# One head row of batch 0 loaded early by SyncE in place of two, in a rotary embedding kernel

## The chip, the cores and the metric

The kernel runs on one core of one Trainium2 chip. The metric is the device time of one execution in microseconds (us); the time of a kernel is the median over several runs.

## The reference

Each pair of halves of a head is rotated by an angle given per position. Everything is float32.

```python
def setup_inputs():
    batch, seq_len, num_heads, head_dim = (8, 2048, 16, 64)
    # x: (8, 2048, 16, 64), cos and sin: (2048, 32), normal draws
def reference(x, cos, sin):
    x1, x2 = x[..., :32], x[..., 32:]
    cos, sin = cos[None, :, None, :], sin[None, :, None, :]
    out1 = x1 * cos - x2 * sin
    out2 = x1 * sin + x2 * cos
    return np.concatenate([out1, out2], axis=-1)
```

The input and the output are 67.1 MB each, so that the kernel moves about 134 MB and does three multiplications or additions for each element.

## The kernel before, in words

The 2048 positions of a batch are spread over 128 partitions with J = 16 consecutive positions in each. One position of one partition, here called a **row**, has 16 heads of 64 elements, that is 4 KB in float32 and 2 KB in float16. A batch is 16 rows in each partition, 64 KB of float32.

The data is kept in float16 in `buf`, five batches deep (NBUF = 5). GpSimd (POOL) issues nearly all transfers, since its software-described DMAs convert between float32 in memory and float16 in `buf`: `load` (the issue is line 71) and `store` (line 81). `in_ring` ties them into one program order, and they all go through one software queue, q0 in the profile, which works first in, first out. A transfer becomes one DMA packet per partition and batch, spread over 16 DMA engines, 8 packets on each, and one closing semaphore packet per engine.

`rotate` (lines 83 to 100) does three VectorE (DVE) operations on a stretch of rows in float16: v = swapped halves times signed sine (line 92), buf = buf times cosine (line 98), buf = buf + v (line 100).

The order of the program is written out by hand (lines 102 to 141):

- SyncE (SP) loads the sine table (line 41) and then the first JA = 2 rows of batch 0, unconverted, into the float32 tile `head` (line 42). ScalarE (ACT) loads the cosine table (line 40). These are hardware-described DMAs, q1 for SP and q10 for ACT.
- POOL issues `load(0)`, which takes rows JA to 15 of batch 0, and `load(1)`.
- ACT converts the tables to float16 (lines 104 to 106) and copies `head` into rows 0 and 1 of `buf` (line 107).
- DVE rotates rows 0 to JA of batch 0 (line 111); POOL stores row 0 alone (line 112), then issues `load(2, 2)` (batches 2 and 3) and `load(4)`.
- DVE rotates the other rows of batch 0 (line 115), and POOL stores rows 1 to 15 (line 116). Batches 1 to 7 follow. A load of batch 5, 6 or 7 waits for the store that frees its buffer.
- At the end, the last two rows of batch 7 leave in another way: ACT copies them to float32 in the same tile `head` (line 134), and SP stores them unconverted (line 135) once the store of rows 0 to 8 of that batch has landed.

Of the kernel before, what the change touches and what calls it, by code (L numbers as in the profile page):

```python
# [1 line left out]

# [4 lines left out]


@with_exitstack  # L10
def kernel(
    ctx: ExitStack,
    tc: tile.TileContext,
    x: bass.AP,
    cos: bass.AP,
    sin: bass.AP,
    out: bass.AP,
):
    nc = tc.nc
    f16 = mybir.dt.float16  # L20
    f32 = mybir.dt.float32

    B, S, H, D = x.shape
    Dh = D // 2
    P = nc.NUM_PARTITIONS
    J = S // P
    NBUF = 5

    const_pool = ctx.enter_context(tc.tile_pool(name="rope_const", bufs=1))
    io_pool = ctx.enter_context(tc.tile_pool(name="rope_io", bufs=1))  # L30
    tmp_pool = ctx.enter_context(tc.tile_pool(name="rope_tmp", bufs=1))

    JA = 2
    head = const_pool.tile([P, JA, H, D], f32)
    x0 = x[0].rearrange("(p j) h d -> p j (h d)", j=J)
    sin_f = const_pool.tile([P, J, Dh], f32)
    cos_f = const_pool.tile([P, J, Dh], f32)
    cos_h = const_pool.tile([P, J, Dh], f16)
    sin_h = const_pool.tile([P, J, D], f16)
    nc.scalar.dma_start(out=cos_f, in_=cos.rearrange("(p j) d -> p j d", j=J))  # L40
    nc.sync.dma_start(out=sin_f, in_=sin.rearrange("(p j) d -> p j d", j=J))
    nc.sync.dma_start(
        out=head.rearrange("p j h d -> p (j h d)"),
        in_=x0[:, 0:JA, :].rearrange("p j f -> p (j f)"),
    )

    buf = io_pool.tile([P, NBUF, J, H, D], f16)

    ring = []

    def in_ring(dma):
        if ring:
            tc.add_manual_dep(
                dma.ins,
                ring[-1].ins.name,
                mybir.DependencyInfo(mybir.DependencyClass.NoSync, mybir.DependencyReason.DATA),
                reason="order of the ring",
            )
        ring.append(dma)
        return dma  # L60

    def load(b, n=1):
        k = b % NBUF
        if n == 1:
            j0 = JA if b == 0 else 0
            dst = buf[:, k, j0:J, :, :].rearrange("p j h d -> p (j h d)")
            src = x[b].rearrange("(p j) h d -> p j (h d)", j=J)[:, j0:J, :].rearrange("p j f -> p (j f)")
        else:
            dst = buf[:, k : k + n, :, :, :].rearrange("p b j h d -> p b (j h d)")
            src = x[b : b + n].rearrange("b (p j) h d -> p b (j h d)", j=J)  # L70
        in_ring(nc.gpsimd.dma_start(out=dst, in_=src))  # L71

    def store(b, n=1, j0=0, j1=J):
        k = b % NBUF
        if n == 1:
            src = buf[:, k, j0:j1, :, :].rearrange("p j h d -> p (j h d)")
            dst = out[b].rearrange("(p j) h d -> p j (h d)", j=J)[:, j0:j1, :].rearrange("p j f -> p (j f)")
        else:
            src = buf[:, k : k + n, :, :, :].rearrange("p b j h d -> p b (j h d)")
            dst = out[b : b + n].rearrange("b (p j) h d -> p b (j h d)", j=J)  # L80
        return in_ring(nc.gpsimd.dma_start(out=dst, in_=src))  # L81

    def rotate(b, j0=0, j1=J):
        v = tmp_pool.tile([P, J, H, D], f16)
        n = j1 - j0
        js = slice(j0, j1)
        xt = buf[:, b % NBUF, js, :, :]
        shape = [P, n, H, 2, Dh]
        sin_b = sin_h[:, js, :].rearrange("p j (e d) -> p j e d", e=2).unsqueeze(2).to_broadcast(shape)
        cos_b = cos_h[:, js, :].unsqueeze(2).to_broadcast([P, n, 2 * H, Dh])  # L90
        xe = xt.rearrange("p j h (e d) -> p j h e d", e=2)
        nc.vector.tensor_mul(  # L92
            out=v[:, js, :, :].rearrange("p j h (e d) -> p j h e d", e=2),
            in0=xe[:, :, :, ::-1, :],
            in1=sin_b,
        )
        xw = xt.rearrange("p j h (e d) -> p j (h e) d", d=Dh)
        nc.vector.tensor_mul(out=xw, in0=xw, in1=cos_b)  # L98
        xa = xt.rearrange("p j h d -> p (j h d)")
        nc.vector.tensor_add(out=xa, in0=xa, in1=v[:, js, :, :].rearrange("p j h d -> p (j h d)"))  # L100

    load(0)
    load(1)
    nc.scalar.copy(out=sin_h[:, :, Dh:D], in_=sin_f)  # L104
    nc.scalar.mul(out=sin_h[:, :, 0:Dh], in_=sin_f, mul=-1.0)  # L105
    nc.scalar.copy(out=cos_h, in_=cos_f)  # L106
    nc.scalar.copy(  # L107
        out=buf[:, 0, 0:JA, :, :].rearrange("p j h d -> p (j h d)"),
        in_=head.rearrange("p j h d -> p (j h d)"),
    )  # L110
    rotate(0, 0, JA)
    store(0, 1, 0, 1)
    load(2, 2)
    load(4)
    rotate(0, JA, J)
    store(0, 1, 1, J)
    rotate(1)
    store(1)
    rotate(2)
    store(2)  # L120
    load(5, 2)
    load(7)
    rotate(3)
    rotate(4)
    store(3, 2)
    rotate(5)
    rotate(6)
    store(5, 2)
    rotate(7)
    gate = store(7, 1, 0, 9)  # L130
    store(7, 1, 9, J - JA)
    last = buf[:, 7 % NBUF, J - JA : J, :, :].rearrange("p j h d -> p (j h d)")
    dst = out[B - 1].rearrange("(p j) h d -> p j (h d)", j=J)[:, J - JA : J, :].rearrange("p j f -> p (j f)")
    nc.scalar.copy(out=head.rearrange("p j h d -> p (j h d)"), in_=last)  # L134
    end = nc.sync.dma_start(out=dst, in_=head.rearrange("p j h d -> p (j h d)"))
    tc.add_manual_dep(
        end.ins,
        gate.ins.name,
        mybir.DependencyInfo(mybir.DependencyClass.Sync, mybir.DependencyReason.DATA),
        reason="the last rows go out behind this part",  # L140
    )


# [1 line left out]
_INS = ['x', 'cos', 'sin']  # L145
_OUTS = [((8, 2048, 16, 64), 'float32')]


# [23 lines left out]
```

## Time and profile before

| what | value |
|---|---|
| time, median of 3 runs | 316.54 us (316.42 to 316.58) |
| the profiled execution: its own time | 316.39 us |
| its span in the profile | 314.6 us |
| DVE busy | 209.1 us, 27 operations |
| ACT busy | 6.7 us |
| POOL busy | 8.6 us |
| HBM read and written | 67.63 MB and 67.11 MB, 428 GB/s over the span |

The profile shows one execution. The span runs from the first to the last event that the profiler recorded; 1.8 us of the execution lie around it. A page gives, for 40 equal slices of the span (7.87 us each), the busy share of each engine in tenths, and the busy share of the core's 16 DMA engines as "DMA". Its bytes per DMA queue count what arrives: float16 for a load of `buf`, float32 for a store. The timeline gives each instruction's start, duration, engine, line and tiles; a DMA issue there is only the issuing instruction, the transfer itself follows later. Windows give the DMA busy share of a stretch, where a packet is put down whole to the window in which it starts. A share above 1 is therefore a window in which many packets start, and a share of 0 is one in which none starts because all engines are still in their packets. Behind these views the trace holds one record per DMA packet, with its queue, start, duration and bytes.

### The profile page before, as it was taken

The numbers are of one execution on the slowest core, as the hardware profiler recorded it, in microseconds if no ns is written. First come the engines' busy times: TensorE is split into PE (matmuls) and PEld (weight loads), VectorE is DVE, ScalarE is ACT, GpSimd is POOL, SyncE is SP. The second block draws the span as 40 slices with busy tenths as digits, with TensorE's granted clock in tenths as the row PEclk, the third lists the DMA queues.
The fourth block names the chain that finished last, engine by engine and source line by source line (L and its number), as shares of the span: only waits on it lengthen the run. The fifth ranks groups of instructions, "written<-read, shape, count | busy, mean of one in ns | idle before, by whom it ended". The sixth has DMA issues, their size and how long they took to land.

```text
span 314.6 us, 114 instructions
## 1 busy us (share of the span) xinstructions
DVE 209.1 (66%) x27; ACT 6.7 (2%) x6; POOL 8.6 (3%) x18
## 2 busy tenths in 40 slices
DVE  0039999992499999999950000899999999910000
ACT  3200000000000000000000000000000000020000
POOL 1020000000000000000010000000000000010000
DMA  7999999999999899999999999999999999999998
GB/s 240 252 242 200 200 267 200 200 267 200 200 200 325 375 500 400 400 400 533 400 200 221 246 200 200 246 221 333 400 508 425 400 400 525 408 400 400 433 425 342
DMA packets 3104, 101.71 MB, mean 323 GB/s; under 512 B 288, under 2 KB 288, under 8 KB 672
## 3 DMA queue, kind: packets, MB, share of 16 engines
q0 software_dynamic: 2528, 99.09, 98.1%
q1 hardware_dynamic: 432, 2.36, 1.9%
q10 hardware_dynamic: 144, 0.26, 0.2%
HBM read 67.63 MB, written 67.11 MB: 428 GB/s over the span
## 4 chain that ended last, share of the span: by engine, by line
DVE 65%; another core or an unknown queue 15%; DMA 7%; ACT 1%; issue 0%; DVEq 0%; ACTq 0%; PEldq 0%
DVE buf L98 22%; DVE v L92 22%; DVE buf L100 22%; DMA buf<-in_x_dram 7%; ACT head L134 1%; DVEq L92 0%; ACTq L134 0%; PEldq L167 0%
## 5 line engine op out<-in xcount | busy, mean ns | idle before, releaser
L92 DVE TENSOR_TENSOR v<-buf,sin_h 128x16384 f16<-128x16384 f16 (+2 forms) x9 | 69.7, 7744 | 66.6 <-DMA buf<-in_x_dram 51.3
L98 DVE TENSOR_TENSOR buf<-buf,cos_h 128x16384 f16<-128x16384 f16 (+2 forms) x9 | 69.7, 7744 | 0.3
L100 DVE TENSOR_TENSOR buf<-buf,v 128x16384 f16<-128x16384 f16 (+2 forms) x9 | 69.7, 7744 | 0.3
L81 POOL DMA_DIRECT2D out_dram<-buf x8 | 4.7, 584 | 219.2 <-DVE buf L100 219.2
L134 ACT CAST head<-buf 128x2048 f32<-128x2048 f16 x1 | 1.9, 1897 | 261.3 <-DVE buf L100 261.3
L71 POOL DMA_DIRECT2D buf<-in_x_dram x6 | 3.7, 628 | 49.7 <-DMA out_dram<-buf 48.9
L107 ACT CAST buf<-head 128x2048 f16<-128x2048 f32 x1 | 1.9, 1897 | 7.1 <-DMA head<-in_x_dram 7.1
L104 ACT ACT_TABLE_LOAD x1 | 1.3, 1283 | 1.2 <-PEq L156 1.2
L104 ACT CAST sin_h<-sin_f 128x512 f16<-128x512 f32 x1 | 0.6, 617 | 2.0 <-DMA sin_f<-in_sin_dram 2.0
L105 ACT ACTIVATE sin_h<-sin_f 128x512 f16<-128x512 f32 x1 | 0.6, 624 | 0.0
L106 ACT CAST cos_h<-cos_f 128x512 f16<-128x512 f32 x1 | 0.6, 601 | 0.0
L156 POOL MEMSET const-float32-0.0<- 128x1 f32 x1 | 0.1, 98 | 0.2 <-issue 0.2
L156 POOL MEMSET const-bfloat16-1.0<- 128x1 bf16 x1 | 0.1, 101 | 0.0
L156 POOL MEMSET const-uint8-127<- 128x1 uint8 x1 | 0.1, 99 | 0.0
L156 POOL MEMSET const-float32-1.0<- 128x1 f32 x1 | 0.1, 98 | 0.0
## 6 DMA issues: line engine op xcount, KB each, us to landing
buf<-in_x_dram POOLq DMA_DIRECT2D x2, 8192.0 KB, 60.3
buf<-in_x_dram POOLq DMA_DIRECT2D x3, 4096.0 KB, 57.4
out_dram<-buf POOLq DMA_DIRECT2D x1, 7680.0 KB, 73.5
out_dram<-buf POOLq DMA_DIRECT2D x1, 4608.0 KB, 28.6
buf<-in_x_dram POOLq DMA_DIRECT2D x1, 3584.0 KB, 22.5
out_dram<-buf POOLq DMA_DIRECT2D x1, 2560.0 KB, 34.1
head<-in_x_dram SPq DMA_DIRECT2D x1, 1024.0 KB, 12.0
out_dram<-head SPq DMA_DIRECT2D x1, 1024.0 KB, 8.4
```

The costliest lines, as they stand in the source:

```text
L71: in_ring(nc.gpsimd.dma_start(out=dst, in_=src))
L81: return in_ring(nc.gpsimd.dma_start(out=dst, in_=src))
L92: nc.vector.tensor_mul(out=v[:, js, :, :].rearrange("p j h (e d) -> p j h e d", e=2), in0=xe[:, :, :, ::-1, :], in1=sin_b,)
L98: nc.vector.tensor_mul(out=xw, in0=xw, in1=cos_b)
L100: nc.vector.tensor_add(out=xa, in0=xa, in1=v[:, js, :, :].rearrange("p j h d -> p (j h d)"))
L104: nc.scalar.copy(out=sin_h[:, :, Dh:D], in_=sin_f)
L105: nc.scalar.mul(out=sin_h[:, :, 0:Dh], in_=sin_f, mul=-1.0)
L106: nc.scalar.copy(out=cos_h, in_=cos_f)
L107: nc.scalar.copy(out=buf[:, 0, 0:JA, :, :].rearrange("p j h d -> p (j h d)"), in_=head.rearrange("p j h d -> p (j h d)"),)
L134: nc.scalar.copy(out=head.rearrange("p j h d -> p (j h d)"), in_=last)
L156: nc = _bacc.Bacc("TRN2", target_bir_lowering=False, num_devices=1)
```

## The change

JA goes from 2 to 1. SP's early load of batch 0 becomes one row (128 packets of 4 KB in place of 8 KB), the software load of batch 0 takes rows 1 to 15 in place of 2 to 15 (60 KB per partition read in place of 56 KB), ACT's copy and the first rotation handle one row in place of two, and the second rotation handles fifteen in place of fourteen. Row 0 is stored alone and rows 1 to 15 together, as before. The tile `head` keeps its two rows and the end of the kernel keeps its two last rows, through a new constant JE = 2.

```diff
-    JA = 2
-    head = const_pool.tile([P, JA, H, D], f32)
+    JA = 1
+    JE = 2
+    head = const_pool.tile([P, JE, H, D], f32)
...
     nc.sync.dma_start(
-        out=head.rearrange("p j h d -> p (j h d)"),
+        out=head[:, 0:JA, :, :].rearrange("p j h d -> p (j h d)"),
         in_=x0[:, 0:JA, :].rearrange("p j f -> p (j f)"),
     )
...
     nc.scalar.copy(
         out=buf[:, 0, 0:JA, :, :].rearrange("p j h d -> p (j h d)"),
-        in_=head.rearrange("p j h d -> p (j h d)"),
+        in_=head[:, 0:JA, :, :].rearrange("p j h d -> p (j h d)"),
     )
     rotate(0, 0, JA)
     store(0, 1, 0, 1)
...
-    store(7, 1, 9, J - JA)
-    last = buf[:, 7 % NBUF, J - JA : J, :, :].rearrange("p j h d -> p (j h d)")
-    dst = out[B - 1].rearrange("(p j) h d -> p j (h d)", j=J)[:, J - JA : J, :].rearrange("p j f -> p (j f)")
+    store(7, 1, 9, J - JE)
+    last = buf[:, 7 % NBUF, J - JE : J, :, :].rearrange("p j h d -> p (j h d)")
+    dst = out[B - 1].rearrange("(p j) h d -> p j (h d)", j=J)[:, J - JE : J, :].rearrange("p j f -> p (j f)")
```

## The prediction, made before the changed kernel was run

> **What bounds the kernel.** I read the page first, for who is busy all the time.
>
> ```profile
> DVE  0039999992499999999950000899999999910000
> ...
> DMA  7999999999999899999999999999999999999998
> ...
> q0 software_dynamic: 2528, 99.09, 98.1%
> q1 hardware_dynamic: 432, 2.36, 1.9%
> q10 hardware_dynamic: 144, 0.26, 0.2%
> ```
>
> The DMA engines are busy from the first slice to the last; DVE rests in some twelve slices. The shares of the queues add up to 100.2% of the span. So the end is set by the sum of the packets' times plus the time in which the engines have no packet. The page's chain of waits puts 65% on DVE, but where two things run side by side it follows only one; the slices decide. Second, the timeline, for what DVE and POOL wait for around the change.
>
> ```profile
> 1.17 0.43 SPq L42 DMA_DIRECT2D head<-in_x_dram  x1
> 1.24 1.21 POOL L71 DMA_DIRECT2D buf<-in_x_dram  x2 [0.80 <-PEq L167]
> ...
> 13.22 1.90 ACT L107 CAST buf<-head 128x2048 f16<-128x2048 f32 x1 [7.11 <-DMA head<-in_x_dram]
> ...
> 19.19 0.54 POOL L81 DMA_DIRECT2D out_dram<-buf  x1 [16.74 <-DVE buf L100]
> ...
> 23.87 7.63 DVE L92 TENSOR_TENSOR v<-buf,sin_h 128x14336 f16<-128x14336 f16 x1 [4.98 <-DMA buf<-in_x_dram]
> ...
> 83.16 8.69 DVE L92 TENSOR_TENSOR v<-buf,sin_h 128x16384 f16<-128x16384 f16 x1 [10.16 <-DMA buf<-in_x_dram]
> ...
> 305.34 0.35 SPq L135 DMA_DIRECT2D out_dram<-head  x1
> ```
>
> DVE begins on batch 0 when its load lands and stands still for 10.16 us before batch 2, again for a load: DVE follows the DMA, not the other way. Third, narrow windows over the first microseconds, since only the start and one queue's sizes change.
>
> ```profile
> 5.00:5.25 0.25, 0.00 (x0) 0.25 (x2) 0.00 (x0) 1.00 1.08 459
> 5.25:5.50 0.25, 0.00 (x0) 0.25 (x1) 0.00 (x0) 1.00 2.21 606
> 5.50:5.75 0.25, 0.00 (x0) 0.25 (x2) 0.00 (x0) 1.00 6.01 1327
> 5.75:6.00 0.25, 0.00 (x0) 0.25 (x1) 0.00 (x0) 1.00 1.06 229
> 6.00:6.25 0.25, 0.00 (x0) 0.11 (x1) 0.00 (x0) 1.00 0.00 0
> ```
>
> The last two columns are DMA share and GB/s. Up to 5.25 a share near 1 is made of short hardware packets; the 6.01 is the start of load(0)'s long packets on most engines. By the packet records each engine does sine and cosine until about 3.6 us, then six of its eight head packets, 0.306 us apart, then (5.49 to 5.93) a load(0) packet, a head packet, a load(0) packet, the last head packet, and load(0) alone.
>
> **The change, part by part.**
>
> 1. *Load(0) grows by a row.* Its packets follow each other every 2.111 us for 14 rows, those of load(1) every 2.413 us for 16: 0.151 us per row and no fixed part that can be seen. Eight packets per engine: +1.21 us.
>
> 2. *Head packets shrink from 8 KB to 4 KB.* On the hardware queues 8 KB packets come every 0.306 us and the tables' 2 KB packets every 0.080 us; a line through both gives 0.155 us for 4 KB. The dearer end is the only 4 KB packet of before, the store of row 0 with its conversion, every 0.187 us. Gain per engine: 8 x (0.306 - 0.155) = 1.21 us, at the dearer end 8 x 0.119 = 0.95. I take 0.155, same queue and direction, and keep 1.50 in place of 1.24 us for all eight as the upper end (+0.26). The two interleaved head packets took 0.319 us, 0.013 more than the others, which gives at most 0.03 back.
>
> So 1 and 2 cancel: the same float32 bytes pass the same engines. The Trainium skill, "DMA: Bandwidth & Descriptors", section "Why small descriptors are slow", speaks against smaller packets: a fixed overhead of about 3 cycles for each. The packet count stays at 3104, so by that rule the sum is unchanged too, and the line above (0.080 to 0.306) has only 0.005 us of fixed part.
>
> 3. *ACT's cast and the first rotation halve.* 1.90 us for 2048 elements and 0.60 for 512 give about 1.03 for 1024; DVE's 1.23 us for 2048 and 7.63 for 14336 give 0.521 ns per element, so 0.69 in place of 1.23, three times. All of it lies beside a busy DMA.
>
> 4. *The second rotation grows* to 15360 elements, 8.16 us in place of 7.63, three times: +1.6 us. It starts at about 23.9 as before, as load(0) plus head is the same work; batch 1 then ends at 74.6 in place of 73.0. DVE waits there until 83.16, so 8.5 us of cover are left. The store of rows 1 to 15 is issued at 48.7 in place of 47.12. It landed 73.5 us after its issue, of which some 18 us are its own transfer: it began at about 102, behind load(4), and 53 us of cover are left. If that cover were gone, the 1.6 us would come in full.
>
> 5. *What is issued earlier.* Head may land between about 5 us (eight short packets in a row) and the old 13, and the store of row 0, with load(2, 2) and load(4) behind it on POOL, is issued that much earlier. In q0 they stand behind load(1), whose packets last until 42.6 us: POOL's queue gets ahead of something that can't start. SP's queue is the same two issues, 0.38 and 0.43 us, and nothing stands behind them until 305.34. The end is not touched (JE = 2).
>
> 6. *The gap that could open.* Before, hardware packets fill the engines until 5.49. With 4 KB packets the six that stood ahead of load(0) are through at 3.65 + 6 x 0.155 = 4.6 us, and all eight at 4.9 (5.15 at 0.187). Does load(0) have its packets ready then? POOL's two issues end at 2.45, and the profile doesn't show readiness. Cost: nothing if ready by 4.6; at the other end, load(0) starts no earlier than 5.49, though no head packet lies between its own any more: +1.21 - 0.64 = +0.57 us. If an empty engine also pays its first read again, 0.669 us for the first table packets that waited against 0.081 for the next, then 0.59 more: +1.16. I take nothing, by the row nearest to it, the end of the kernel:
>
> ```profile
> 305.25:305.50 0.25, 0.00 (x0) 0.00 (x0) 0.00 (x0) 1.00 2.38 983
> ...
> 309.75:310.00 0.25, 0.00 (x0) 0.00 (x0) 0.00 (x0) 1.00 2.38 983
> 310.00:310.25 0.25, 0.00 (x0) 0.00 (x0) 0.00 (x0) 1.00 0.79 328
> 310.25:310.50 0.25, 0.00 (x0) 0.00 (x0) 0.00 (x0) 1.00 0.00 0
> 310.50:310.75 0.25, 0.00 (x0) 0.00 (x0) 0.00 (x0) 1.00 1.15 393
> ```
>
> SP issues the last store at 305.34, and still the software store's 0.75 us packets start in rounds until 309.75 to 310.25; only at 310.5 do the short hardware packets begin. Their first issue, at 0.74 us, had its first packet at 1.74, so the hardware packets were very likely ready at about 306.4, and four or five whole software packets on each engine went first. An engine thus works off several packets that it had taken in before another queue's. By that reading load(0) was ready when six head packets stood ahead of it, on all 16 engines alike although their head packets began anywhere from 3.65 to 4.10 us, and those six now pass in half the time.
>
> **The sum,** against the profiled execution's 316.39 us (span 314.6 and 1.8 around it): +1.21 - 1.21 = 0, with -0.03 to +0.26 for the packets: 316.4 to 316.7. The median of the runs is 0.15 higher, so **316.6 us** for the median.
>
> **The rivals.**
>
> *A: the gap opens* (slower). Load(0) becomes ready only at about 5.4 us, and the engines stand idle from 4.9 on. For it: its first packet came 4.2 us after POOL's issue, and 14 of 16 engines would fit one moment of readiness at 5.41 to 5.49. Against it: two engines started a head packet at 5.62 and fit only a later moment, and the end of the kernel shows a queue that had to wait for packets already taken in. It decides from 4.9 us on. Price +0.57 to +1.16: 317.1 to 317.7, middle 317.4 us. The same page, section "Queues, rings and completion order", says that an engine goes round-robin between its queues at packet granularity; taken strictly, six head packets in a row mean that load(0) wasn't there, which is this rival. The end of the kernel does not agree, with four or five packets of one queue first. Its "Specifications" give a software DMA about 1 us to the first byte, which would have load(0) ready by an estimated 2.9 us and no gap; no row here shows that.
>
> *B: head doesn't come earlier* (the change doesn't do what it says). If load(0) stood in turn with every head packet, the last of eight would be through at 3.65 + 8 x 2.42 = 23 us, and the first rotation would push the second back by 2 to 4 us. The 8.5 us of cover hold that: 316.6 us.
>
> *C: faster.* Software packets move a row in 0.151 us, hardware ones in 0.153: 0.02 us over eight. A gain of 0.6 would have to come out of the start's wait for the first read (1.74 to 2.5 us), which the change leaves alone. 315.8 us if it did; nothing in the profile is for it.
>
> **Chances.** A difference of 0.2% (0.63 us) is about what a measurement of this kernel can tell from no change. Forecast 0.57, A 0.34, B 0.03, C 0.06. Of A, 0.04 lies below 317.17 and so within 0.2%. Faster 0.06, within 0.64, slower 0.30. The range goes from 316.2 to 317.5: it leaves out C and the upper third of A (0.11).
>
> **What the profile of the changed kernel would show.** Steps 1 and 2: 3104 packets, those under 8 KB from 672 to 800; load(0) packets 2.26 us apart. Step 4: DVE's second stretch at 23.9 and its wait before batch 2 about 8.5 us. Step 6: narrow windows from 4.5 to 5.5 us at share 1 or above, with load(0)'s first packets at about 4.6; for A, windows near 0 between 4.9 and 5.5. I am wrong if such a hole stands there, if 4 KB head packets come at 0.187 us or more, or if the time moves by more than 0.6 us with none of these.

## The result and the profile after

The changed kernel took **317.16 us** (median of 15 runs, 317.04 to 317.59), the kernel before 316.58 us on the same chips (15 runs, 316.41 to 316.78). The ratio is 1.0021, 95% interval 1.0014 to 1.0028: slower, by 0.58 us (0.18%) between the medians. The profiled execution of the changed kernel took 317.04 us, 0.65 more than that of before (316.39).

The page of the changed kernel first: the rows for DVE and DMA in 40 slices, the packets and the queues.

```profile
DVE  0109999995399999999950000899999999910000
...
DMA  9899999999999999999999999999999999999997
...
DMA packets 3104, 101.45 MB, mean 322 GB/s; under 512 B 288, under 2 KB 288, under 8 KB 800
...
q0 software_dynamic: 2528, 99.35, 98.3%
q1 hardware_dynamic: 432, 1.84, 1.5%
```

The packets are as foretold: 3104, with those under 8 KB up from 672 to 800. The DMA is still the bound. Next the timeline, where each line gives start, duration, engine, line and tiles, and in brackets the wait.

```profile
1.16 0.42 SPq L43 DMA_DIRECT2D head<-in_x_dram  x1
...
6.04 1.04 ACT L108 CAST buf<-head 128x1024 f16<-128x1024 f32 x1 [0.22 <-DMA head<-in_x_dram]
...
9.55 0.54 POOL L82 DMA_DIRECT2D out_dram<-buf  x1 [7.11 <-DVE buf L101]
...
24.23 8.16 DVE L93 TENSOR_TENSOR v<-buf,sin_h 128x15360 f16<-128x15360 f16 x1 [14.98 <-DMA buf<-in_x_dram]
...
83.80 8.69 DVE L93 TENSOR_TENSOR v<-buf,sin_h 128x16384 f16<-128x16384 f16 x1 [8.85 <-DMA buf<-in_x_dram]
```

Row 0 lands 7 us earlier (its cast starts at 6.04 in place of 13.22) and nothing comes of it. But load(0) lands 0.36 us later (24.23 against 23.87), and DVE's wait before batch 2 ends 0.64 later (83.80 against 83.16): nearly the whole loss is there after a quarter of the span. The narrow windows over the start say where; the last two columns are DMA share and GB/s. First three windows of the kernel before:

```profile
3.75:4.00 0.25, 0.00 (x0) 0.00 (x0) 0.00 (x0) 1.00 1.05 434
4.00:4.25 0.25, 0.00 (x0) 0.00 (x0) 0.00 (x0) 1.00 0.90 377
4.25:4.50 0.25, 0.00 (x0) 0.04 (x1) 0.00 (x0) 1.00 1.24 524
```

The changed kernel from the same moment on:

```profile
3.75:4.00 0.25, 0.00 (x0) 0.00 (x0) 0.00 (x0) 1.00 1.33 336
4.00:4.25 0.25, 0.00 (x0) 0.09 (x1) 0.00 (x0) 1.00 0.70 197
4.25:4.50 0.25, 0.00 (x0) 0.25 (x1) 0.00 (x0) 1.00 0.84 311
4.50:4.75 0.25, 0.00 (x0) 0.25 (x2) 0.00 (x0) 1.00 1.07 426
4.75:5.00 0.25, 0.00 (x0) 0.25 (x2) 0.00 (x0) 1.00 3.62 926
5.00:5.25 0.25, 0.00 (x0) 0.25 (x2) 0.00 (x0) 1.00 3.34 811
5.25:5.50 0.25, 0.00 (x0) 0.25 (x2) 0.00 (x0) 1.00 1.84 418
5.50:5.75 0.25, 0.00 (x0) 0.25 (x1) 0.00 (x0) 1.00 1.75 385
```

There is no hole between 4.9 and 5.5; by the packet records no engine stands empty from 4.51 us to the end (from 3.7 to 4.5 the gaps of all 16 together are 0.45 us). But from 3.75 to 4.5 the rate is 336, 197 and 311 GB/s, where it was 434, 377 and 524: packets start and take long. By the packet records, 26 of the 128 head packets take over 0.2 us, the worst 0.76, against 0.16 for an undisturbed one. The last 58, which start from 4.52 us on, all take 0.16 again. Load(0)'s first packets, which before started within 0.45 us of each other on the 16 engines, are now strewn from 4.89 to 5.71.

The packet records of the two profiles, by stage, with the first and the last of the 16 engines (the records name no engine, so that the two can be different engines from stage to stage):

| start of the stage, us | before | after |
|---|---|---|
| load(0) | 5.49 to 5.93 | 4.89 to 5.71 |
| load(1) | 23.04 to 23.49 | 23.05 to 23.85 |
| second half of load(2, 2) | 63.13 to 63.45 | 63.25 to 64.10 |
| end of the last packets | 313.09 to 313.41 | 313.20 to 314.06 |

Each engine works off its own packets and is never idle, so one that falls behind at 4 us is not helped by the others, and the spread is still there at the end. The first engine to end loses 0.11 us, the mean 0.25, the last 0.65, and the last is the time: in all 14 profiles of this study the execution's time is the end of the last packet plus 2.98 or 2.99 us. The mean does not tell it: in the run without an early row, below, the mean end is 313.45 as in the changed kernel, but the last engine ends at 313.66 and the profiled execution took 316.64 us.

### The profile page after: what moved, and what is told of

It is laid out like the page before. It is cut to its first block, busy times and chain, and to the rows that moved or that the text cites. A ratio compares the mean times of both kernels' runs of the same rounds, so it can differ in the third digit from the quotient of the medians.

```text
span 315.3 us, 114 instructions
## 1 busy us (share of the span) xinstructions
DVE 209.1 (66%) x27; ACT 5.9 (2%) x6; POOL 8.6 (3%) x18
## 2 busy tenths in 40 slices
DMA packets 3104, 101.45 MB, mean 322 GB/s; under 512 B 288, under 2 KB 288, under 8 KB 800
## 4 chain that ended last, share of the span: by engine, by line
DVE 66%; another core or an unknown queue 14%; DMA 7%; ACT 1%; issue 0%; DVEq 0%; ACTq 0%; PEldq 0%
DVE buf L99 22%; DVE v L93 22%; DVE buf L101 22%; DMA buf<-in_x_dram 7%; ACT head L135 1%; DVEq L93 0%; ACTq L135 0%; PEldq L168 0%
## 5 line engine op out<-in xcount | busy, mean ns | idle before, releaser
L108 ACT CAST buf<-head 128x1024 f16<-128x1024 f32 x1 | 1.0, 1044 | 0.2 <-DMA head<-in_x_dram 0.2
```

The source lines that it names most:

```text
L108: nc.scalar.copy(out=buf[:, 0, 0:JA, :, :].rearrange("p j h d -> p (j h d)"), in_=head[:, 0:JA, :, :].rearrange("p j h d -> p (j h d)"),)
```

## The experiments

Theory 1 at the outset was that 4 KB packets leave too little under way when load(0)'s reads begin; theory 2 that each such packet simply costs more; theory 3 is rival A, load(0) not ready; theory 4 blames the longer packets of the fifteen-row load. Theories 5 and 6, on memory addresses, came out of the first runs. All medians stand against the kernel before on the same chip.

| run | median us | ratio to before, 95% interval | load(0) starts on the engines | load(1)'s last engine starts | last packet ends |
|---|---|---|---|---|---|
| no early row | 316.59 | 1.0001 (0.9992 to 1.0010) | 3.77 to 4.07 | 23.39 | 313.66 |
| 8 KB packets, one row unused | 317.85 | 1.0044 (1.0031 to 1.0057) | 5.37 to 5.92 | 24.88 | 314.75 |
| two rows as 2 x 4 KB | 317.36 | 1.0026 (1.0017 to 1.0035) | 5.06 to 5.80 | 24.14 | 314.10 |
| head row ahead of sine | 316.93 | 1.0013 (1.0004 to 1.0022) | 5.16 to 5.81 | 23.99 | 313.85 |
| row steps of 4 KB | 316.61 | 1.0002 (0.9993 to 1.0011) | 4.90 to 5.22 | 23.37 | 313.58 |
| row steps of 68 KB | 316.52 | 1.0000 (0.9991 to 1.0009) | 4.92 to 5.34 | 23.45 | 313.39 |
| row steps of 32 KB | 316.54 | 1.0002 (0.9993 to 1.0010) | 4.99 to 5.44 | 23.56 | 313.50 |
| row steps of 128 KB | 316.55 | 1.0001 (0.9992 to 1.0010) | 5.01 to 5.37 | 23.49 | 313.56 |
| steps of 64 KB, batch 4 | 317.20 | 1.0021 (1.0012 to 1.0030) | 5.12 to 5.85 | 24.00 | 314.21 |
| eight memsets | 317.21 | 1.0023 (1.0013 to 1.0032) | 4.99 to 5.65 | 23.81 | 314.17 |
| load(0) held back | 317.51 | 1.0036 (1.0024 to 1.0049) | 4.91 to 5.72 | 24.10 | 314.37 |
| batch 0 stored whole | 317.34 | 1.0023 (1.0014 to 1.0032) | 4.91 to 5.71 | 23.83 | 314.10 |

**No early row.**

```diff
-    nc.sync.dma_start(out=head[...], in_=x0[:, 0:JA, :]...)
...
-        j0 = JA if b == 0 else 0
+        j0 = 0
...
-    nc.scalar.copy(out=buf[:, 0, 0:JA, :, :]..., in_=head[:, 0:JA, :, :]...)
```

> No early head row at all: the software load of batch 0 takes all sixteen rows, row 0 is still rotated and stored alone first. Theory 1 (short packets run dry: load(0) is ready at about 4 us, and its first reads catch the 4 KB head packets with too little in flight): load(0)'s first packets start between 3.6 and 4.4 us, right behind the tables, and the time is that of before to 0.3 us, 316.6 to 316.9. Theory 2 (each 4 KB packet simply costs 0.188 us): no such packets, 316.6. Theory 3 (rival A of the prediction, load(0) ready only at about 4.9 to 5.4 us): the engines stand idle from 3.7 to then, and the time is 317.8 to 318.4.

The windows of this run, at the end of the tables:

```profile
3.50:3.75 0.25, 0.00 (x0) 0.00 (x0) 0.00 (x0) 1.00 1.10 426
3.75:4.00 0.25, 0.00 (x0) 0.00 (x0) 0.00 (x0) 1.00 8.47 1901
4.00:4.25 0.25, 0.00 (x0) 0.00 (x0) 0.00 (x0) 1.00 1.83 393
```

All 16 first packets of load(0) start in these last two windows, right behind the tables. With the same POOL issue as ever, load(0) is ready at 3.77 us or sooner, long before the 4.9 at which rival A begins. That rival and theory 3 fall. And the early row buys nothing at all: without it the time is that of before.

**8 KB packets with one row unused.** This run moves row 1 of batch 0 twice.

```diff
-        out=head[:, 0:JA, :, :].rearrange("p j h d -> p (j h d)"),
-        in_=x0[:, 0:JA, :].rearrange("p j f -> p (j f)"),
+        out=head[:, 0:JE, :, :].rearrange("p j h d -> p (j h d)"),
+        in_=x0[:, 0:JE, :].rearrange("p j f -> p (j f)"),
```

> The changed kernel, but SyncE loads two rows (8 KB packets) of which only the first is used, so that row 1 is moved twice: 0.52 MB more, 8 x 0.151 = 1.21 us per engine. Theories 1 and 2 (the loss lies in the 4 KB packets): the loss of 0.58 goes, 316.58 + 1.21 = 317.8, and the engines' starts of load(0) lie within 0.45 us of each other as before. Theory 4 (the loss lies in the longer packets of the fifteen-row load): 317.16 + 1.21 = 318.4.

317.85 us: the extra bytes and little more. By the medians 0.09 us go beyond the 1.21, by the interval -0.2 to 0.6, so that this run alone does not rule out a loss of 0.58. The starts of load(0) lie 0.55 us apart, more than the 0.45 foretold. That the longer packets of the fifteen-row load (theory 4) are not the cause is settled by the four runs with other steps below: they have the same load and lose nothing.

**Two rows as two DMAs of 4 KB packets**, in the kernel before.

```diff
-    nc.sync.dma_start(
-        out=head.rearrange("p j h d -> p (j h d)"),
-        in_=x0[:, 0:JA, :].rearrange("p j f -> p (j f)"),
-    )
+    for j in range(JA):
+        nc.sync.dma_start(
+            out=head[:, j : j + 1, :, :].rearrange("p j h d -> p (j h d)"),
+            in_=x0[:, j : j + 1, :].rearrange("p j f -> p (j f)"),
+        )
```

> The kernel before, with its two head rows in two DMAs of one row each: the same bytes, sixteen 4 KB packets per engine in place of eight of 8 KB. Theory 2: 16 x 0.188 - 8 x 0.309 = +0.54 on every engine, 317.1. Theory 1: packets at about 0.155 apart except for one hole at about 4.0 to 4.5 us, where some engines lose 0.1 to 0.6; 316.8 to 317.2, the engines spread by 0.6 or more. Theory 3: hardware packets last past 5.4 us, no gap, 316.6.

The same bytes as before, and 0.26% slower. Most packets of the first row follow each other at 0.155 us; ten of 256 take 0.2 to 0.5, all started between 3.9 and 4.8 us; the 172 that start later take at most 0.17. Theory 2 (an even price) does not fit such a scatter; theory 1 does, though the time lies above what either foretold.

**The head row ahead of the sine table.**

```diff
-    nc.sync.dma_start(out=sin_f, ...)
     nc.sync.dma_start(out=head[:, 0:JA, ...], ...)
+    nc.sync.dma_start(out=sin_f, ...)
```

> The changed kernel with SyncE's two issues exchanged: the head row goes ahead of the sine table, so that 2 KB table packets are under way at 4 us. Theory 1: the hole at 4.0 to 4.5 us stays at its time and falls on the sine packets; the time stays at 317.0 to 317.4. Theory 2: the 4 KB packets cost 0.188 at their new place too, no hole at 4.0 to 4.5; 316.8 to 317.2. Theory 3: the hardware packets end when they did, at about 4.9, so 317.2 again.

A miss for theory 1. The 2 KB sine packets under way from 4.5 us on run undisturbed; the long ones (27 over 0.2 us, up to 1.19) are the 4 KB head packets again, now started between 1.7 and 3.6 us, the earlier ones being the first reads of all. Smaller packets do not suffer, so it is not shortness alone. What sets the head's packets apart from the tables' is their addresses: table packets lie 2 KB apart in memory, head packets 64 KB. This led to theory 5.

**Other steps between the early rows.** Four runs of the changed kernel read the same number of 4 KB packets from other rows of the input.

```diff
-        in_=x0[:, 0:JA, :].rearrange("p j f -> p (j f)"),
+        in_=x[0, 0:P].rearrange("s h d -> s (h d)"),                              # 4 KB apart
+        in_=x.rearrange("b s h d -> (b s) (h d)")[0 : 17 * P, :]
+            .rearrange("(p j) f -> p j f", j=17)[:, 0, :],                       # 68 KB; 8: 32 KB, 32: 128 KB
```

> The changed kernel, but the early 4 KB packets come from 128 neighbouring rows of memory (4 KB apart) in place of rows 64 KB apart; row 0 of each partition thus holds other positions' data, so that part of batch 0 is not what the reference computes. Theory 5 (the stall comes from memory: 128 reads of 4 KB at 64 KB steps hit the same part of it, the slowest engine waits longest): the stall of 0.1 to 0.6 us goes, 316.6 to 316.7, engines' starts of load(0) within 0.45 us. Theory 1 (short packets leave too little in flight, wherever they come from): the stall stays, 317.1 to 317.2, spread 0.6 or more.

> As the run with neighbouring rows, but with the 4 KB rows 68 KB apart (again other positions' data in row 0 of batch 0). Theory 5: spread over memory by the odd step, 316.6 to 316.7. Theory 1: 317.1 to 317.2.

> As the run with neighbouring rows, with the early rows 32 KB apart (other positions' data in row 0 of batch 0). Theory 5, if what counts is a large power of two in the step: 317.0 to 317.2 again, or half of it, 316.8 to 316.9, if half the step meets twice as many parts of the memory. If only the step of 64 KB, shared with load(0), counts (theory 6): 316.5 to 316.7.

> As the run with neighbouring rows, with the early rows 128 KB apart (other positions' data in row 0 of batch 0). Theory 5: as slow as 64 KB or slower, 317.1 to 317.8, spread 0.7 or more. Theory 6: half of the rows lie in other batches' addresses, 316.6 to 316.9.

The run with steps of 4 KB, in the same windows as above:

```profile
3.75:4.00 0.25, 0.00 (x0) 0.00 (x0) 0.00 (x0) 1.00 1.06 426
4.00:4.25 0.25, 0.00 (x0) 0.01 (x1) 0.00 (x0) 1.00 0.99 410
4.25:4.50 0.25, 0.00 (x0) 0.25 (x1) 0.00 (x0) 1.00 1.11 459
4.50:4.75 0.25, 0.00 (x0) 0.25 (x1) 0.00 (x0) 1.00 0.91 377
4.75:5.00 0.25, 0.00 (x0) 0.25 (x2) 0.00 (x0) 1.00 6.40 1507
5.00:5.25 0.25, 0.00 (x0) 0.25 (x1) 0.00 (x0) 1.00 3.59 803
```

The rate stays at 377 to 459 GB/s where it fell to 197, and load(0) starts on all engines in two windows in place of four. In all four runs each of the 128 head packets takes 0.16 us and the time is that of before: the whole loss is gone, with packet size, count, destination and queues unchanged. So the loss is in where the packets read. Theory 5 was right for 4 and 68 KB, but wrong in its simple form: 32 and 128 KB are large powers of two as well and show nothing. What is left is the step that load(0) has too.

**Steps of 64 KB in another batch.**

```diff
-        in_=x0[:, 0:JA, :].rearrange("p j f -> p (j f)"),
+        in_=x[4].rearrange("(p j) h d -> p j (h d)", j=J)[:, 0:JA, :].rearrange("p j f -> p (j f)"),
```

> The changed kernel with its early 4 KB rows taken at the same 64 KB steps, but from batch 4 in place of batch 0, 33.6 MB away from what load(0) reads (row 0 of batch 0 thus holds batch 4's data, which is not what the reference computes). Steps of 4, 32, 68 and 128 KB showed no stall, and a later load(0) moved part of it into load(0)'s own first packets. Theory 6a (head rows and load(0)'s packets lie in the same 64 KB blocks and get into each other's way there): no stall, 316.5 to 316.7, engines' starts of load(0) within 0.45 us. Theory 6b (equal steps of 64 KB meet the same parts of the memory, wherever they lie): the stall stays, 317.0 to 317.3, spread 0.6 or more.

Its windows:

```profile
3.75:4.00 0.25, 0.00 (x0) 0.00 (x0) 0.00 (x0) 1.00 1.46 467
4.00:4.25 0.25, 0.00 (x0) 0.00 (x0) 0.00 (x0) 1.00 0.79 311
...
5.75:6.00 0.25, 0.00 (x0) 0.25 (x1) 0.00 (x0) 1.00 0.57 123
```

The dip is back (311; milder, with 9 packets over 0.2 us in place of 26), load(0)'s last start falls behind 5.75, and the time is 1.0021 again. The nearness of the head rows to load(0)'s is not needed (theory 6a falls); the step of 64 KB is (6b).

**Load(0) later.** Two runs asked whether load(0)'s own reads, at the same steps, take part.

```diff
+    idle = const_pool.tile([P, 128], f32)          # the first run
+    for _ in range(8):
+        nc.gpsimd.memset(idle, 0.0)
...
+    nc.gpsimd.memset(buf[:, 0, JA:J, :, :].rearrange("p j h d -> p (j h d)")[:, 0:1536], 0.0)   # the second
     load(0)
```

> The changed kernel with eight small memsets on POOL ahead of load(0), so that its issue comes about 0.5 to 1 us later. Theory 1 (load(0)'s first long reads, taken in at about 4 us, hold the head's short ones up): the stall moves later by as much or vanishes, as the short packets are then read before the long ones come; 316.6 to 316.9 as long as load(0) is ready by 4.9. Theory 5: the stall stays at 4.0 to 4.5, 317.1 to 317.3. Theory 3 (load(0) is ready just in time): a gap as long as the delay, 317.7 to 318.2.

> The changed kernel with a memset by POOL on part of load(0)'s own destination, so that load(0) must be issued behind it, about 1 us later than before (the run with eight small memsets moved it by 0.03 us only). Theory 5 (4 KB reads at 64 KB steps are slow by themselves): the stall stays on the head packets at 4.0 to 4.5 us, the engines' starts of load(0) spread by 0.6 or more, 317.1 to 317.4. Theory 6 (such reads are slow only while load(0)'s first long reads, at the same 64 KB steps, are under way too): the stall goes or comes about 1 us later, the spread falls to 0.45 or less, 316.6 to 316.8; if load(0) is not ready at 4.9, a gap adds up to 0.3 us to either.

The first failed as an experiment: the memsets were put between and behind the issues, load(0) went out at 1.27 us in place of 1.24, and the time is that of the changed kernel. In the second it went out at 2.42. Long head packets are fewer (5 over 0.2 us in place of 26), while three of load(0)'s own first packets now take 2.5 to 2.8 us in place of 2.28; the spread stays at 0.81, and the time, 317.51, lies above what either theory foretold. Load(0) starts at 4.91 us as in the changed kernel, though it went out 1.2 us later: a further sign against rival A. Part of the stall moved on to load(0)'s reads with it, as theory 6 has it, and part stayed, as theory 5 has it. One profile does not settle the shares.

**Batch 0 stored whole.**

```diff
-    store(0, 1, 0, 1)
...
-    store(0, 1, 1, J)
+    store(0, 1, 0, J)
```

> The changed kernel without the separate store of row 0: batch 0 goes out as one store of sixteen rows. The start is untouched, so the lag of the slowest engine at load(0) (0.36 more than before) stays. If the other part of the profile's difference (0.28 us, at the change from load(1) to the store of row 0) is tied to that store, it goes: 316.8 to 316.95. If it is only a matter of the one profiled execution, or is paid at any change from loads to stores: 317.1 to 317.2.

317.34 us, no gain: the loss is not tied to the store of row 0.

## Why the prediction was right and wrong

The time lies in the range (316.2 to 317.5), but above the forecast of 316.6, and the loss (0.18% by the medians, 0.21% by the ratio) lies on the bound between "within 0.2%" and "slower". That the range holds it is luck: its upper part was kept for rival A, which did not happen, and the sum itself gave at most 316.7 for the profiled execution, which took 317.04.

- **What bounds the kernel, steps 1, 3, 4, 5 and rival B: right.** Load(0)'s undisturbed packets follow every 2.26 us as worked out; the second rotation takes 8.16 us; the cover before batch 2 shrank from 10.16 to 8.85 us (8.5 foretold); the earlier row and POOL's earlier issues change nothing.
- **Step 2 failed: "I take 0.155, same queue and direction".** The mean over all head packets was 0.188 us (1.51 us for eight, the upper end kept for the range), though undisturbed ones take 0.159 and follow each other every 0.155. The prediction's own sign, 4 KB packets at 0.187 us or more, is met by this mean, but by stalls and not by an even price. The line was drawn through the tables' packets, whose rows lie side by side in memory, and through 8 KB packets; neither is a 4 KB read at steps of 64 KB. The runs with other steps show the difference at equal size.
- **The sum failed in a second way: it was made for a mean engine.** The mean end moved by 0.25 us, within the +0.26 kept for the packets. The slowest moved by 0.65, and the slowest is the time. Not counted was that a stall hits the engines unevenly and that nothing later evens it out.
- **Step 6 was right, and rival A right only in its number.** There is no gap: load(0) is ready by 3.77 us, and its packets follow the last head packet at once on every engine. A's 317.1 to 317.7 holds the result by another mechanism. The Trainium skill, "DMA: Bandwidth & Descriptors", section "Queues, rings and completion order", has each engine take turns between its queues at packet granularity, a packet there being typically 9 to 17 descriptors (single copy orders). If a record of the profile is one such descriptor, as no run here shows, eight head packets in a row are less than one turn, and rival A's strict reading does not follow from the page. If a record is a whole packet of the page, the trace does not agree: with load(0) ready by 3.77, all eight head packets still went first in the changed kernel. In the kernel before, six went first and then single records of both queues took turns, which fits neither reading.

Of the cause this is shown: the loss needs 4 KB head packets at steps of 64 KB. They are not enough by themselves: in the changed kernel those from 4.52 us on run undisturbed at the same size and step. The same page of the Trainium skill, section "Latency and other measured facts", tells of copies of rows that lie large powers of two apart (207 GB/s at 512 KiB, 164 at 2 MiB, 103 at 4 MiB), cured at 4 MiB by 4 KiB more. The run at 68 KB agrees; those at 32 and 128 KB do not, so a power of two by itself is not the rule here.

Open is how the memory turns this step into a stall, and how much load(0)'s equal step adds. A smaller part of the loss comes later: the four profiles with head packets at 64 KB steps and load(0) at its old time (changed kernel, batch 4, eight memsets, batch 0 whole) have the slowest engine start load(1) at 23.87 on average, against 23.46 for the six without the stall (before, no early row, the four other steps), 0.41 later; at the end it is 314.14 against 313.52, 0.62 later. In the profiles of before and after, the packet records put the further lag into one packet, the slowest engine's last of load(1), just ahead of the store of row 0: 2.53 us before, 2.81 after, where the other packets of load(1) take 2.43. It does not belong to the stall alone: the same packet takes 2.83 us in the run with no early row and 2.81 at steps of 4 KB, and 2.57 with two rows as 2 x 4 KB, which has the stall. Against the first two of these, the changed kernel's profile loses 0.40 and 0.48 us in place of 0.65. What makes this packet longer or shorter was not found.

No version beat the kernel before: with the 16 engines never empty from load(0) on and the bytes fixed, the variants without the stall all end at 316.5 to 316.6 us.

## What to carry to other kernels

Where the DMA engines are never idle, a short stall in the first microseconds is not made good later, and the slowest engine's lag is the loss: look at the spread of the engines, not at their mean. Price a smaller packet by its addresses as well as by its size; a row next to it in size may read quite another pattern of memory. A load that lands earlier is worth nothing where the engine that waits for it has 8 us to spare.

## What the runs showed of the hardware that was not expected

- 128 reads of 4 KB at steps of 64 KB: 0.188 us per packet on average, up to 0.76, all the long ones started before 4.52 us; at steps of 4, 32, 68 and 128 KB: 0.159 each, 0.155 apart. 8 KB packets at 64 KB steps, 0.306 apart, showed little of it: none over 0.36 us before, and at the start of the run with one row unused three of 128 at 0.42 to 0.65.
- Packets of one queue can go first in a row although another queue is ready: eight 4 KB packets ahead of a load that was ready by 3.77 us. At the end of the kernel before, four or five software packets on each engine went ahead of a hardware store that was ready at about 306.4 us, an estimate from its issue at 305.34 and the 1.0 us that the first hardware DMA took from issue to first packet.
- The last packets of load(1), just ahead of the store of row 0, take longer than the others: on the slowest engine 2.47 to 2.97 us in the 13 profiles with that store, against 2.43 for the packets before them, and 2.43 where row 0 has no store of its own.
- The time of an execution is the end of its last DMA packet plus 2.98 to 2.99 us in every profile.
